# Hybrid decoder trunk: the splitting of the down projection's weights planned ahead, and two additions of squares moved from GpSimd to VectorE

## The chip, the cores and the metric

The kernel runs on one core of a Trainium2 chip. The time is the device time of one execution in microseconds. Before the change the median of 3 runs is 2677.97 us (2677.93 to 2678.42). One more execution was profiled; all durations come from that one.

The engines are called as in the profile: PE (TensorE, matmul), PEld (its weight loads), DVE (VectorE), ACT (ScalarE), POOL (GpSimd) and SP (SyncE, which here only starts DMAs; its queue is SPq).

## The reference

Two layers over 1024 tokens of width 1024. Each is a mixer (attention, gates, output projection) and a gated feed-forward part; a last RMSNorm follows. The part that matters here is the feed-forward one:

```python
h2 = rmsnorm(x, norm2[l])
up = h2 @ w_up[l]                         # 1024 -> 2 x 2816
a, v = up[..., :D_FF], up[..., D_FF:]
a = causal_depthwise_conv(a, conv_w[l], conv_b[l])   # width 3
x = x + (jax.nn.gelu(a, approximate=False) * v) @ w_down[l]   # 2816 -> 1024
```

and the first RMSNorm of the next layer, which needs the mean of the squares of `x` over its 1024 features. All is float32.

## The kernel before

**Numbers in two parts.** Every float32 operand of a matmul is kept as a high and a low part: ACT casts the high part (`split`, L134), DVE subtracts it from the original to get the low part (L139), and PE does three matmuls for each product (high x high, high x low, low x high). A "weight piece" below is one 128x512 block of weights in these two parts.

**Blocks with seven products.** The up and the down projection multiply 2x2 blocks with seven products in place of eight (Strassen's scheme in Winograd's form). It needs sums and differences of weight blocks (on POOL and DVE) and of the gated activations.

**The up projection** runs over 22 units `j`, each 128 of the 2816 features: seven products on PE, then `conv` (an ACT pass, two DVE passes L1338 and L1339, and a GELU on ACT), `gated` (DVE, L1364), differences on POOL (L1369), and `spill`: each result is split (tile `g`, DVE L139) and stored to memory (`gd`), seven stores for each pair of units. Of the last unit these parts are written into the first steps of the down projection, through `at(...)`, which runs them so many turns later.

**The down projection** (`down`) runs over 28 steps `s`: four groups of 2, 2, 3 and 4 pieces of the inner dimension, times seven products `k`. So group 0 is steps 0 to 6 and group 1 steps 7 to 13. In each step:
- `load_g` fetches activations (`gd_in`) some steps ahead; `load_raw` fetches raw weights (`wd_raw`, 1 MB each) at steps 3, 7 and 14 for the following group;
- `prep(s)` prepares weight pieces up to three steps ahead: POOL's L1601 and L1604, DVE's L1605 and L1608 form the sums and differences, and `split` makes the two parts, in buffers `w_hi`/`w_lo` (four) or, from group 1 on, `wd` (tag `p4`, four);
- `product_of(s, e)` for four output blocks `e`: the matmuls (L1630 to L1632, 6 to 12 of 512 columns) into a PSUM bank, and then DVE adds the bank into `x` (L1638).

Steps with `k` = 1, 2, 3 accumulate into the banks that the step before has used, and `k` = 6 into those of `k` = 5. So the first matmul of a block there must wait until DVE has added that block of the step before.

The four `p4` buffers are shared at this place by the last unit's conv tile `cv` (held until its last spill), by the spills' `g` (held until the store has ended) and by `wd`.

**The norm between the layers.** `norm_add` squares a block of `x` on ACT (L424) and adds it to a running sum (L426). The addition is DVE's for every third block and POOL's for the others, unless the argument `adds` says which. In `enter`, `second()` runs the last two steps (`k` = 5 and 6) for the second half of the tokens; after them PE sums over features with `nrm_t` matmuls (L473), behind the next layer's value projection (`v_ps`).

**What sets the order.** PE's order is the written one everywhere. For ACT, DVE and POOL it is the written one within the up projection and in what step 0 of the down projection issues up to its first block; further on, a planner at build time simulates the program and gives each engine, of the instructions that are ready, the one with the lowest number. The number is the place in the program; inside `tc.high_priority(offset=AHEAD)` an instruction counts as if written 200 instructions (`AHEAD`) earlier. An instruction that needs a buffer which is taken waits, and others pass it. On the chip each engine then follows its fixed order. Before the change the additions into `x` (L1638) have this priority, and nothing of `prep` has it.

Of the kernel before, what the change touches and what calls it, by code (L numbers as in the profile page):

```python
# [7 lines left out]
F32R = mybir.dt.float32r  # L8
# [7 lines left out]
P = 128  # L16
# [3 lines left out]
HF = 512  # L20
# [27 lines left out]
AHEAD = 200  # L48
# [3 lines left out]
def f32(ap):  # L52
    return ap.bitcast(F32)
# [3 lines left out]
def trunk_kernel(ctx, tc, x, norm1, w_in, b_gate, w_br, w_o, norm2, w_up, conv_w, conv_b, w_down, norm_f, out, depth=None, probe=None):  # L57
    nc = tc.nc
    act, dve, pe, pool = nc.scalar, nc.vector, nc.tensor, nc.gpsimd
# [4 lines left out]
    sb = ctx.enter_context(tc.tile_pool(name="sb", bufs=1))  # L64
# [56 lines left out]
    def small(name, dtype=F32):  # L121
        return sb.tile([P, 512], dtype, tag="pt", bufs=PT, name=name)
# [8 lines left out]
    def split(hi, lo, src, turn=None):  # L131


        one = act.copy(hi, src)  # L134
        if turn == "is":
            LAST["act"] = one.ins.name
        elif turn == "waits" and LAST:
            tc.add_manual_dep(one.ins, LAST["act"], NO_SYNC, reason="in turn")
        two = dve.tensor_tensor(lo, src, f32(hi), ALU.subtract)  # L139
        if turn == "is":  # L140
            LAST["dve"] = two.ins.name
# [31 lines left out]
    def drive(side, main, ratio, lead=0):  # L173

        due = 0.0
        for _ in range(lead):
            next(main, 0)
        for _ in side:
            due += ratio
            while due >= 1.0:  # L180
                due -= 1.0
                if next(main, 0) == 0:
                    due = -1e9
        for _ in main:
            pass
# [213 lines left out]
    def xc(n, e, sub=slice(0, HF)):  # L399
        return X[n][e // 4][:, e % 4, sub]  # L400

    def x_move(n, out):
        for h in range(2):
            there = xs[n][:, 4 * h : 4 * h + 4, :]
            nc.sync.dma_start(*((there, X[n][h]) if out else (X[n][h], there)))
# [11 lines left out]
    def norm_add(n, e, first=False, sub=slice(0, HF), adds=None):  # L417

        if first:
            ACC[n] = sb.tile([P, HF], F32, tag="ql", bufs=2, name="nrm")  # L420
        acc = ACC[n]
        acc = acc[:, sub]
        sq = acc if first else small("sq")[:, sub]
        act.activation(sq, xc(n, e, sub), AF.Square)  # L424
        if not first:
            (adds or (dve if e % 3 == 1 else pool)).tensor_tensor(acc, acc, sq, ALU.add)  # L426
# [40 lines left out]
    def norm(n, gain, tag, then=None, keep=False):  # L467
        acc = ACC[n]
        ss = sb.tile([P, 8], F32, tag="ss", bufs=2, name="ss")
        yield  # L470
        tot = bank(tag, "nrm_t")
        for c in range(4):
            pe.matmul(tot[:, c : c + 1], acc[:, c * P : (c + 1) * P], ones, start=True, stop=True, skip_group_check=True)  # L473
        yield
        act.activation(ss[:, 0:4], tot[:, 0:4], AF.Sqrt, bias=eps[:, 0:1], scale=1.0 / D)
        dve.reciprocal(ss[:, 4:8], ss[:, 0:4])
        if then:
            table(then, ss[:, 4:5])
        yield
        rb = bank(tag, "nrm_b")  # L480
        for c in range(4):
            pe.transpose(rb[:, c * P : (c + 1) * P], ss[:, 4 + c : 5 + c].to_broadcast([P, P]), ident)
        yield
        new_h(n)
        for e in range(KD):
            hf = kept_f32(n, e) if keep else small("hf")
            dve.scalar_tensor_tensor(hf, xc(n, e), gain[:, e : e + 1], rb, ALU.mult, ALU.mult)
            hi, lo = H[n][0][:, e, :], H[n][1][:, e, :]
            act.copy(hi, hf)
            (pool if e % 2 and not (keep and n) else dve).tensor_tensor(lo, hf, f32(hi), ALU.subtract)  # L490
            if e < KD - 1:
                yield
# [79 lines left out]
    def head(l):  # L572


        def place(n, name):
            x = [big(name, F32R) for _ in range(n)]
            return ([x[0][:, h, :] for h in range(2)] if n == 1 else [y.rearrange("p a b -> p (a b)") for y in x])

        wv = weights(w_in[l][:, OFF_VB : OFF_VB + 256], 256, place(2, "v_w")) if l else early.pop("wv")
        others = lambda: [weights(w_in[l][:, off : off + P], P, place(1, "kq_w")) for off in (OFF_KB, OFF_QB)]  # L580
        if l:
            wk, wq = others()
        yield
        vt = R["vb"] = new_v("vb")
        kt = R["kb", 0] = big("kt", F32R)
        q = R["qb", 0] = new_q()
        if l:
            yield from values_part(vt, wv, range(2))
        else:
            yield from values_part(vt, wv, range(1))  # L590
            wk, wq = others()
            yield from values_part(vt, wv, range(1, 2))
        for n in range(2):
            yield from keys_half(kt, wk, n)
            yield from queries_half(q, wq, n, SCALE)
            if n == 0 and not l:
                yield from values_part(vt, wv, range(2, 4))
        if l:
            yield from values_part(vt, wv, range(2, 4))
# [319 lines left out]
    def piece(src, turn=None):  # L919
        hi = sb.tile([P, 512], F32R, tag="wh", bufs=4, name="w_hi")  # L920
        lo = sb.tile([P, 512], F32R, tag="wl", bufs=4, name="w_lo")
        split(hi, lo, src, turn)
        return hi, lo
# [385 lines left out]
    def ffn(l, pending, final):  # L1309
# [237 lines left out]
        def down(box):  # L1547
# [31 lines left out]
            def place(s, g):  # L1579

                used = [tag for v in range(s, state["w"] + 1) for tag, _ in ws.get(v, ())]
                for tag in ("p4", "w") if g else ("w",):
                    if used.count(tag) < 4:
                        return tag

            def prep(s, most=3):

                while state["w"] < min(s + most, count):
                    v = state["w"]
                    g, k = flat[v]  # L1590
                    m = GROUPS[g]
                    used = [tag for u in range(s, v) for tag, _ in ws[u]]
                    room = 4 - used.count("w") + (4 - used.count("p4") if g else 0)
                    if room < m or (g, m - 1) not in raws:
                        return
                    ws[v] = []
                    for i in range(m):
                        a11, a12, a21, a22 = raws[g, i]
                        if k == 0:
                            temps[i] = small("wd_s")  # L1600
                            pool.tensor_tensor(temps[i], a11, a21, ALU.subtract)  # L1601
                            src = a11
                        elif k == 1:
                            pool.tensor_tensor(a21, a21, a22, ALU.add)  # L1604
                            dve.tensor_tensor(a11, a21, a11, ALU.subtract)  # L1605
                            src = a11
                        elif k == 6:
                            dve.tensor_tensor(a11, a12, a11, ALU.subtract)  # L1608
                            src = a11
                        else:  # L1610
                            src = {2: temps[i], 3: a22, 4: a12, 5: a21}[k]
                        tag = place(s, g)
                        if tag == "p4":
                            w = sb.tile([P, 2, HF], F32R, tag="p4", bufs=4, name="wd")
                            w = (w[:, 0, :], w[:, 1, :])
                            split(*w, src)
                        else:
                            w = piece(src)
                        ws[v].append((tag, w))
                    state["w"] += 1  # L1620

# [27 lines left out]
            for _ in range(READY - 3):  # L1649
                yield  # L1650
            prep(0, 1)
            yield
            yield
            for s, (g, k) in enumerate(flat):
# [8 lines left out]
                elif s == 14:  # L1663
                    for i in range(3):
                        load_raw(3, i, "e8")
                    load_raw(3, 3, "ql")
                prep(s)
                main, other = ("t", "o"), ("ps", "s")
                if g % 2:
# [40 lines left out]
    def enter(l):  # L1710


        def go(rest):
            x_move(0, True)
            heads[l] = [head(l)]
            next(heads[l][0])

            def second():
                for k in (5, 6):
                    for e in range(4):  # L1720
                        yield from rest(k, e)
                        norm_add(1, e + 4 * (k == 5), k == 5 and e == 0)

            drive(norm(0, g1[:, 0, :], "t"), second(), SECOND, 3)
            x_move(1, True)
            return norm(1, g1[:, 0, :], "s", AF.Sigmoid)

        return go
# [271 lines left out]
```

## Time and profile before

| | |
|---|---|
| median of 3 runs | 2677.97 us |
| the profiled execution's own time | 2679.46 us |
| its span in the profile | 2677.4 us |
| granted TensorE clock | 0.999 |
| busy: PE, PEld | 2654.8 us (99%), 2228.7 us (83%) |
| busy: DVE, ACT, POOL | 2031.8 (76%), 1352.3 (51%), 643.7 us (24%) |
| down projection, first layer | from 1129.76 us on |
| down projection, second layer | from 2451.58 us on |
| DMA in group 0, first layer (1129.76 to 1169.50) | 346 GB/s, 94% of the engines' time |

How to read the lines in this text: a timeline row has the start in us from the start of the span, the duration in us, the engine, the line of the kernel, the operation, the tile written and the tiles read, the shape, and in square brackets the idle time before it and what ended it. A row of waits has who waited for whom, the us in total, the number of times and the longest. A row of a stretch has its borders and length, then busy us and number of instructions for PE, PEld, DVE, ACT and POOL, the granted clock, the share of DMA and GB/s. Matmuls are pipelined, so that their recorded durations overlap.

### The profile page before, as it was taken

The page shows a single profiled execution, that of the slowest core. Times are in us where ns is not written, and L with a number is a line of the kernel's source. Part 1 is how long each engine was busy: PE and PEld are TensorE (multiplying, and loading weights), DVE is VectorE, ACT ScalarE, POOL GpSimd, SP SyncE. Part 2 cuts the span into 40 slices and gives each one's busy share as a digit, 9 for nine tenths or more (in the row PEclk, how much of TensorE's full clock was granted, in tenths as well). Part 3 has the DMA queues.
Part 4 walks back from the last instruction along what each step waited for, and adds up shares of the span by engine and source line. Part 5 has one row for each costly group of instructions (what it writes and reads, how often), then busy time and mean ns, then how long its engine had stood idle before and what let it go on. Part 6 is the DMA issues. An engine that isn't in the chain of part 4 may idle for free.

```text
span 2677.4 us, 36661 instructions
## 1 busy us (share of the span) xinstructions
PE 2654.8 (99%) x13080; PEld 2228.7 (83%) x13080; DVE 2031.8 (76%) x3089; ACT 1352.3 (51%) x2494; POOL 643.7 (24%) x467
## 2 busy tenths in 40 slices
PE   9999999999999999999999999999999999999999
PEld 8988888888888888888889888888788888888888
DVE  6777756685888988897658777566858888898865
ACT  6656645464545554532435565455635555554225
POOL 1003211122233443321210041111321344343210
PEclk9999999999999999999999999999999999999999
DMA  5212178573244444688411122785732544446863
GB/s 182 56 55 87 49 196 248 192 251 109 78 138 152 166 141 152 225 317 317 160 36 44 48 79 88 216 246 182 231 95 71 165 150 148 159 157 249 335 249 119
DMA packets 364354, 424.19 MB, mean 158 GB/s; under 512 B 20756, under 2 KB 293516, under 8 KB 362124
## 3 DMA queue, kind: packets, MB, share of 16 engines
q1 hardware_dynamic: 364156, 421.85, 47.9%
q8 instruction: 103, 1.69, 0.3%
q14 instruction: 79, 0.65, 0.1%
q10 hardware_dynamic: 16, 0.00, 0.0%
HBM read 278.07 MB, written 143.72 MB: 158 GB/s over the span
## 4 chain that ended last, share of the span: by engine, by line
PE 88%; DVE 6%; DMA 2%; ACT 2%; issue 1%; POOL 0%; DVEq 0%; SPq 0%; ACTq 0%; POOLq 0%
PE u_a L928 5%; PE u_a L930 5%; PE u_a L929 5%; PE d_ps L1630 5%; PE d_ps L1631 5%; PE d_ps L1632 5%; PE i_a L928 3%; PE u_c L928 3%; PE u_c L930 3%; PE u_c L929 3%; PE i_a L929 3%; PE i_a L930 2%; PE o_ps L166 2%; PE o_ps L168 2%; PE o_ps L167 2%; PE g_ps L166 2%
## 5 line engine op out<-in xcount | busy, mean ns | idle before, releaser
L139 DVE TENSOR_TENSOR w_lo<-up_a,w_hi 128x512 fp32r<-128x512 f32 x240 | 236.9, 994 | 20.5 <-ACT w_hi L134 20.5
L134 ACT CAST w_hi<-up_a 128x512 fp32r<-128x512 f32 x240 | 149.4, 622 | 184.9 <-PE u_a L929 45.8
L1638 DVE TENSOR_TENSOR x<-x,d_ps 128x512 f32<-128x512 f32 (+1 forms) x228 | 152.4, 673 | 77.7 <-PE d_ps L1632 76.5
L1369 POOL TENSOR_TENSOR cv<-cv 128x512 f32<-128x512 f32 x88 | 131.8, 1508 | 249.4 <-DVE cv L1364 139.5
L139 DVE TENSOR_TENSOR g<-cv,g 128x512 fp32r<-128x512 f32 x154 | 151.3, 984 | 5.3 <-ACT g L134 2.8
L139 DVE TENSOR_TENSOR w_lo<-w_raw,w_hi 128x512 fp32r<-128x512 f32 x144 | 110.3, 769 | 56.4 <-ACT w_hi L134 56.0
L134 ACT CAST w_hi<-w_raw 128x512 fp32r<-128x512 f32 x144 | 89.4, 621 | 115.8 <-PE o_ps L167 67.3
L139 DVE TENSOR_TENSOR w_lo<-in_a,w_hi 128x512 fp32r<-128x512 f32 x120 | 90.6, 755 | 60.0 <-ACT w_hi L134 54.5
L134 ACT CAST w_hi<-in_a 128x512 fp32r<-128x512 f32 x120 | 74.5, 621 | 118.3 <-PE i_c L929 49.0
L1630 PE MATMUL d_ps<-gd_in,w_hi 128*128 128x512 f32 (+1 forms) x340 | 130.5, 384 | 1.3 <-ACT w_hi L134 0.6
L1632 PE MATMUL d_ps<-gd_in,w_lo 128*128 128x512 f32 (+1 forms) x340 | 130.0, 382 | 0.0
L1631 PE MATMUL d_ps<-gd_in,w_hi 128*128 128x512 f32 (+1 forms) x340 | 129.9, 382 | 0.0
L928 PE MATMUL u_a<-hh,w_hi 128*128 128x512 f32 x320 | 124.8, 390 | 0.8 <-DVE u L1520 0.8
L928 PE MATMUL u_a<-t_hi,w_hi 128*128 128x512 f32 x320 | 124.7, 390 | 0.0
L929 PE MATMUL u_a<-hl,w_hi 128*128 128x512 f32 x320 | 124.7, 390 | 0.0
L930 PE MATMUL u_a<-hh,w_lo 128*128 128x512 f32 x320 | 124.7, 390 | 0.0
L930 PE MATMUL u_a<-t_hi,w_lo 128*128 128x512 f32 x320 | 124.7, 390 | 0.0
L929 PE MATMUL u_a<-t_lo,w_hi 128*128 128x512 f32 x320 | 124.6, 390 | 0.0
L134 ACT CAST g<-cv 128x512 fp32r<-128x512 f32 x154 | 94.9, 616 | 42.0 <-POOL cv L1369 29.4
L658 DVE TENSOR_TENSOR_SCAN stay<-stay,zero 128x512 f32<-128x512 f32 (+2 forms) x96 | 93.5, 974 | 28.7 <-ACT stay L645 28.1
L1630 PE MATMUL d_ps<-gd_in,wd 128*128 128x512 f32 (+1 forms) x292 | 114.0, 390 | 0.0
L1632 PE MATMUL d_ps<-gd_in,wd 128*128 128x512 f32 (+1 forms) x292 | 112.9, 387 | 0.0
(410 smaller groups left out, 8609.7 us busy)
## 6 DMA issues: line engine op xcount, KB each, us to landing
gd<-g SPq DMA_DIRECT2D x154, 512.0 KB, 3.3
gd_in<-gd SPq DMA_DIRECT2D x154, 512.0 KB, 6.5
up_a<-in_w_up_dram SPq DMA_DIRECT2D x80, 512.0 KB, 5.2
t_kq<-tk SPq DMA_DIRECT2D x32, 768.0 KB, 5.7
wd_raw<-in_w_down_dram SPq DMA_DIRECT2D x22, 1024.0 KB, 7.3
w_raw<-in_w_in_dram SPq DMA_DIRECT2D x80, 256.0 KB, 3.2
in_a<-in_w_in_dram SPq DMA_DIRECT2D x40, 512.0 KB, 4.9
gin<-gs SPq DMA_DIRECT2D x32, 512.0 KB, 4.2
```

What stands on the lines that cost most here:

```text
L134: one = act.copy(hi, src)
L139: two = dve.tensor_tensor(lo, src, f32(hi), ALU.subtract)
L166: pe.matmul(o, lh, rh, start=(first and i == 0), stop=False, skip_group_check=share)
L658: one = dve.tensor_tensor_scan(rev, rev, zero[:, 0:1].to_broadcast([P, c1 - c0]), 1.0 if c1 == L else sv[:, c1 : c1 + 1], ALU.mult, ALU.add)
L928: pe.matmul(o, w[0][:, c], rh, start=(first and i == 0), stop=False, skip_group_check=True)
L929: pe.matmul(o, w[0][:, c], rl, start=False, stop=False, skip_group_check=True)
L930: pe.matmul(o, w[1][:, c], rh, start=False, stop=(last and i == 3), skip_group_check=True)
L1369: return lambda: pool.tensor_tensor(dst, a, b, ALU.subtract)
L1630: pe.matmul(o[:, sub], wh[:, c], gh[:, sub], start=(i == 0 and k in (0, 4, 5)), stop=False, skip_group_check=True)
L1631: pe.matmul(o[:, sub], wh[:, c], gl[:, sub], start=False, stop=False, skip_group_check=True)
L1632: pe.matmul(o[:, sub], wl[:, c], gh[:, sub], start=False, stop=(i == m - 1), skip_group_check=True)
L1638: dve.tensor_tensor(x, x, o[:, sub], ALU.add)
```

## The change

The splitting of the down projection's weights into two parts (a cast on ACT, a subtraction on DVE) gets the same priority of 200 places; the indented lines are otherwise the same. The sums and differences of weight blocks before it (L1601, L1604, L1605, L1608) stay outside. In `enter`, for the norm between the layers, the additions of squares of the last two blocks of the last step (`k` = 6, `e` = 2 and 3) go to DVE; by the rule for every third block both were POOL's.

```diff
+from contextlib import nullcontext
...
                         tag = place(s, g)
-                        if tag == "p4":
-                            w = sb.tile([P, 2, HF], F32R, tag="p4", bufs=4, name="wd")
-                            w = (w[:, 0, :], w[:, 1, :])
-                            split(*w, src)
-                        else:
-                            w = piece(src)
+                        with tc.high_priority(offset=AHEAD) if True else nullcontext():
+                            if tag == "p4":
+                                w = sb.tile([P, 2, HF], F32R, tag="p4", bufs=4, name="wd")
+                                w = (w[:, 0, :], w[:, 1, :])
+                                split(*w, src)
+                            else:
+                                w = piece(src)
                         ws[v].append((tag, w))
...
-                        norm_add(1, e + 4 * (k == 5), k == 5 and e == 0)
+                        norm_add(1, e + 4 * (k == 5), k == 5 and e == 0, adds=dve if k == 6 and e > 1 else None)
```

## The prediction

> **What bounds the kernel now.** I read the page's busy table first, then the list of who waited for whom on PE, then the busy time by stretches, and last the timelines of PE, DVE, ACT and POOL around each place where PE waits in the code that the diff touches.
>
> ```profile
> span 2677.4 us, 36661 instructions
> ...
> PE 2654.8 (99%) x13080; PEld 2228.7 (83%) x13080; DVE 2031.8 (76%) x3089; ACT 1352.3 (51%) x2494; POOL 643.7 (24%) x467
> ```
>
> ```profile
> PE br_ps L166 <- DVE gin L1284: 2.5, 3, 1.2
> ...
> PE d_ps L1630 <- ACT w_hi L134: 0.6, 2, 0.3
> PE nrm_t L473 <- POOL nrm L426: 0.5, 1, 0.5
> ```
>
> ```profile
> 1129.76:1169.50 39.74, 38.91 (x169) 31.31 (x168) 39.51 (x57) 15.55 (x25) 10.55 (x7) 1.00 0.94 346
> ...
> 1207.60:1264.70 57.10, 57.10 (x253) 47.33 (x252) 40.37 (x59) 15.05 (x26) 11.65 (x8) 1.00 0.84 313
> ```
>
> ```profile
> L1638 DVE TENSOR_TENSOR x<-x,d_ps 128x512 f32<-128x512 f32 x26 | 17.5, 680 | 0.2
> ```
>
> PE is busy for 99% of the span, and its waits in the code of the change are tenths of a microsecond. So whatever this change can win is small, and a loss needs a new stall. The rows, in order: the page's span and busy times; three of PE's waits (us in total, times, longest); two stretches of the program; and the additions into x within the first of these. The two rows of stretches (length, then PE, PEld, DVE, ACT, POOL busy) hold the main point. In the first, group 0 of the down projection of the first layer (steps 0 to 6), DVE is busy for 39.51 of 39.74 us: for this stretch VectorE, and not PE, sets the pace. In group 2, with three weight pieces to a step, DVE is at 40.37 of 57.10 and an order among its instructions costs nothing. The second layer repeats the first.
>
> What those waits cost is read best from the starts of successive matmuls, because a recorded matmul (0.39 us) is longer than the distance to the next.
>
> ```profile
> 1134.74 0.39 PE L1631 MATMUL d_ps<-gd_in,w_hi 128*128 128x512 f32 x1
> 1134.97 0.39 PE L1632 MATMUL d_ps<-gd_in,w_lo 128*128 128x512 f32 x1
> 1135.65 0.47 PE L1630 MATMUL d_ps<-gd_in,w_hi 128*128 128x512 f32 x1 [0.29 <-ACT w_hi L134]
> ...
> 1162.75 0.39 PE L1632 MATMUL d_ps<-gd_in,w_lo 128*128 128x512 f32 x1
> 1163.55 0.47 PE L1630 MATMUL d_ps<-gd_in,w_hi 128*128 128x512 f32 x1 [0.41 <-issue]
> ...
> 1164.78 0.40 PE L1632 MATMUL d_ps<-gd_in,w_lo 128*128 128x512 f32 x1
> 1165.31 0.50 PE L1630 MATMUL d_ps<-gd_in,w_hi 128*128 128x512 f32 x1
> ...
> 1348.22 0.28 PE L167 MATMUL v_ps<-v_w,hh 128*128 128x256 f32 x1
> 1348.34 0.28 PE L168 MATMUL v_ps<-v_w,hl 128*128 128x256 f32 x1
> 1349.11 1.05 PE L473 MATMUL nrm_t<-ones,nrm 128*128 128x1 f32 x8 [0.49 <-POOL nrm L426]
> ...
> 2456.80 0.39 PE L1632 MATMUL d_ps<-gd_in,w_lo 128*128 128x512 f32 x1
> 2457.47 0.47 PE L1630 MATMUL d_ps<-gd_in,w_hi 128*128 128x512 f32 x1 [0.29 <-ACT w_hi L134]
> ...
> 2486.02 0.39 PE L1632 MATMUL d_ps<-gd_in,w_lo 128*128 128x512 f32 x1
> 2486.54 0.50 PE L1630 MATMUL d_ps<-gd_in,w_hi 128*128 128x512 f32 x1
> ```
>
> An undisturbed matmul follows after 0.23 us (1134.74 to 1134.97). The excess is 0.68 - 0.23 = 0.45 at step 1, 0.80 - 0.23 = 0.57 and 0.53 - 0.23 = 0.30 at step 6, together 1.32 in the first layer. In the second it is 0.44 and 0.29, together 0.73. The 256-wide matmuls follow after 0.12, so the norm's sum waits 0.77 - 0.12 = 0.65. All that the diff could remove is therefore 1.32 + 0.73 + 0.65 = 2.70 us, 0.1% of the span.
>
> **The change, part by part.** No instruction is added or removed but two that change engine. First, the splitting of the down projection's weights: the casts on ACT (L134) and the subtractions on DVE (L139) get the same 200 places that the additions into x (L1638) have. The sums and differences before them (L1601 and L1604 on POOL, L1605 and L1608 on DVE) stand outside the block and keep their number. The split instructions pass the convolution, the GELU and the spills of the last up unit, and also those additions into x that are written behind them.
>
> ```profile
> 1132.48 1.27 DVE L1339 SCALAR_TENSOR_TENSOR cv<-u,cw,cv 128x1022 f32<-128x1022 f32 x1
> 1133.67 0.68 DVE L1638 TENSOR_TENSOR x<-x,d_ps 128x512 f32<-128x512 f32 x1
> 1134.27 0.68 DVE L139 TENSOR_TENSOR w_lo<-wd_raw,w_hi 128x512 fp32r<-128x512 f32 x1
> 1134.87 1.88 DVE L1638 TENSOR_TENSOR x<-x,d_ps 128x512 f32<-128x512 f32 x3
> ...
> 1159.77 0.68 DVE L139 TENSOR_TENSOR g<-cv,g 128x512 fp32r<-128x512 f32 x1
> ...
> 1162.77 0.68 DVE L1638 TENSOR_TENSOR x<-x,d_ps 128x512 f32<-128x512 f32 x1
> 1163.37 0.68 DVE L139 TENSOR_TENSOR w_lo<-wd_raw,w_hi 128x512 fp32r<-128x512 f32 x1
> 1163.97 0.68 DVE L139 TENSOR_TENSOR wd<-wd_raw,wd 128x512 fp32r<-128x512 f32 x1
> 1164.57 0.68 DVE L1638 TENSOR_TENSOR x<-x,d_ps 128x512 f32<-128x512 f32 x1
> ```
>
> Step 1. The gap at 1135.65 is put down to ACT, but the cast that the w_lo of 1134.27 reads was over by then; PE starts 0.1 us after a DVE addition (the second, 1134.87 + 0.60, as 1163.37 to 1163.97 shows one DVE operation taking 0.60 of the queue). My reading is that output block 0's addition, written behind step 1's weights by hand, had to let another block's addition (1133.67) pass ahead of the second w_lo (1134.27). With equal priority the w_lo comes first, everything behind it moves up by 0.60, and the 0.45 goes: in both layers 0.89. I take this as likely to happen.
>
> Step 6. Four additions a step, 26 in the stretch: the one at 1162.77 is the 21st, block 0 of step 5. Step 6 accumulates into the same banks, so the matmul at 1163.55 must wait for it (1162.77 + 0.68 = 1163.45), and the one at 1165.31 for the 22nd (1165.25). These times are fixed by how much DVE work is queued ahead, since DVE has no idle time from 1129.76 on (0.23 us in all). So the 0.45 that PE gains at step 1 is waited for again at step 6, and is worth nothing there unless DVE gets less to do before these additions. That is the step I weigh most: step 1 nets 0, and not -0.89.
>
> What can leave the queue ahead of them are spills (g, 1159.77: 0.60 each, not read before group 3), because the weights take their buffers first:
>
> ```profile
> 1158.24 0.62 ACT L134 CAST wd<-wd_raw 128x512 fp32r<-128x512 f32 x1 [0.66 <-DMA gd<-g]
> ...
> 1160.48 0.62 ACT L134 CAST wd<-wd_raw 128x512 fp32r<-128x512 f32 x1 [0.50 <-DVE g L139]
> ```
>
> ```profile
> 1155.71 1.29 POOL L1601 TENSOR_TENSOR wd_s<-wd_raw 128x512 f32<-128x512 f32 x1 [5.21 <-DMA wd_raw<-in_w_down_dram]
> ```
>
> Here wd waits, and g before it, for the same four buffers (tag p4) until an earlier g has been written to memory. With the new priority the last two spills can lose to step 7's weights: up to 2 x 0.60 = 1.2 us less ahead of the 22nd addition, the gain's bound. What can pass the 21st are step 6's second w_lo and step 7's wd (1163.37, 1163.97): it ends 1.2 later, block 0 of step 6 starts at 1164.75 and block 1, six matmuls of 0.23 on, at 1166.1 in place of 1165.31, a loss of 0.8. The 22nd itself already stands behind both. So step 6 moves by -1.2 to +0.8 in a layer; I take the middle, -0.2, since the queue is full whichever comes first: -0.4 in both layers. SP: no load is moved by hand; the spills' stores come later with their casts, and nothing on the queue behind them reads them before group 3. A weight block that lands late (POOL waited 5.21 us for it) limits how early step 7's second piece can go. Groups 2 and 3 have DVE time to spare, so I cost the edit there at nothing; were it full, the price would be 0.60 per addition passed.
>
> Second, the two additions of squares.
>
> ```profile
> 1346.29 0.68 DVE L1638 TENSOR_TENSOR x<-x,d_ps 128x512 f32<-128x512 f32 x1
> 1347.00 0.63 ACT L424 ACTIVATE sq<-x 128x512 f32<-128x512 f32 x1 [1.38 <-DVE x L1638]
> 1347.78 1.28 POOL L426 TENSOR_TENSOR nrm<-nrm,sq 128x512 f32<-128x512 f32 x1 [2.56 <-ACT sq L424]
> ```
>
> The last one ends the chain x, square, sum, matmul at 1349.11. On DVE it takes 0.68 for 1.28: -0.60 of the 0.65 wait. The one before it costs DVE 0.60 while DVE waits for loads, so nothing on the path; were it queued ahead of 1346.29 it would cost its 0.60 and leave no gain. I take -0.60.
>
> The Trainium skill (SBUF — State Buffer, section SBUF: two separate sides) says that a VectorE operation with two SBUF inputs and a GpSimd operation lock each other out for a whole instruction. The trace has such longer times: 1.62 for a subtraction whose like take 0.68 (the row of 1177.76 further down). By that rule taking POOL's additions away would also shorten DVE's subtractions beside them, the norm would give its whole 0.65, and the sum would be less by 0.05.
>
> Sum: step 1 -0.89, given back at step 6 +0.89, step 6's own -0.4, norm -0.60: -1.0 us. The profiled execution took 2679.46 us around its 2677.4 of span, 1.5 above the median of 2677.97; against that median the sum gives 2677.0.
>
> **The rivals.** First, the change does all that its words say: PE's waits at steps 1 and 6 go as well. For it speaks that spills leave the queue; against it that DVE is at 39.51 of 39.74. Time: 2677.97 - 2.70 = 2675.3.
>
> Second, on the other side: the spills starve. If step 7's two pieces and step 8's first hold three of the four p4 buffers while the last conv tile holds the fourth until its last spill, then step 8's second piece gets a buffer only when step 7 is nearly over.
>
> ```profile
> 1174.28 0.39 PE L1630 MATMUL d_ps<-gd_in,wd 128*128 128x512 f32 x1
> ...
> 1175.64 0.39 PE L1630 MATMUL d_ps<-gd_in,wd 128*128 128x512 f32 x1
> 1177.76 1.62 DVE L139 TENSOR_TENSOR wd<-wd_raw,wd 128x512 fp32r<-128x512 f32 x1
> ```
>
> Step 7's first piece is read last before 1174.28. Then come a cast of 0.62, up to three queued operations of 0.60 and a subtraction of 0.68 to 1.62: ready at 1175.6 to 1178.3, wanted at 1175.64 + 2 x 0.23 = 1176.1. So it costs 0 to 2.2 us in a layer, 4.4 in both; with step 6's worst case (2 x 0.8) and the norm's gain, 4.4 + 1.6 - 0.6 = +5.4, 2683.4. It decides from the moment at which three weight pieces have p4 buffers and one spill has none. That weights and spills already wait for one another there speaks for it; that the second block's load lands late, so that the spills may slip in, speaks against. A row of such waits is what the Trainium skill (Perfetto Trace Analysis, section Optimization Strategy) would put down to too few buffers, a gap that comes back on an engine that should be full; by it a new order leaves the gaps, and this rival with its 2683.4 gains on the first.
>
> Third, the planner, fed other times, orders the next layer's mixer otherwise. The longest single wait of PE in the list is 1.2 us (for gin, in the mixer); one such wait more or less is its price, 2675.8 or 2678.2 with the sum above.
>
> **How the numbers follow.** My sum has 0.45, with its own range 2675.6 to 2679.2 (step 6 at -1.2 or +0.8 in one layer and half of it in the other, the norm's 0.60 kept at the low end and lost at the high one); the first rival 0.22, the starved spills 0.25, the third 0.08. The time is that of the likeliest, 2677.0. The range goes from 2674.9, just under the first rival, to 2682.5, within the second, of which some 0.10 lies above. A measurement of this kernel tells about 0.2%, 5.4 us, from no change. Faster than 2672.6 is out of reach of the 2.70 found: 0.03, left to the third rival, whose single wait may be several. Slower than 2683.3: half of the second, since its 2683.4 has step 8 alone and step 11 has the same pair of pieces, 0.12, and 0.03 of the third: 0.15. Within: 0.82.
>
> **What would show it.** Right: no gap at step 1, a gap of much the same sum at step 6, DVE full up to step 8, the nrm_t matmul straight behind v_ps with a DVE addition of 0.68 ahead of it. Wrong on the fast side: no gap at step 6 and spills' g behind its additions. Wrong on the slow side: PE waiting at steps 8 or 11 for a wd cast or subtraction, which waited for a buffer from step 7, or a wait of DVE for a block that has not landed.

## The result and the profile after

| | before | after |
|---|---|---|
| median | 2677.36 us (2674.94 to 2679.99, 22 runs) | 2680.53 us (2677.78 to 2685.97, 22 runs) |
| ratio | 1 | 1.0012, interval 1.0007 to 1.0018 |
| profiled execution, its span | 2679.46, 2677.4 us | 2680.04, 2677.9 us |

The change makes the kernel slower by 3.2 us (1.9 to 4.8 by the interval). I had forecast 2677.0, a gain of 1.0, in a range from 2674.9 to 2682.5. The measured time lies in the range and within 0.2% of before, but the sign is the other one.

The runs spread over 5 us before and 8 us after, and in the two profiled executions parts of the program that the change does not touch differ by some 2 us. So the traces are compared by stretches: the table gives distances in time on PE, from the first matmul of the down projection to step 6 and to step 14 (the end of group 1), and the sum of the gaps in between (a distance of two matmuls less the undisturbed 0.23 us, where this is over 0.09).

| | step 6 at, layer 1 / 2 | step 14 at, layer 1 / 2 | gaps by step, layer 1 | gaps by step, layer 2 |
|---|---|---|---|---|
| before | 33.79 / 33.21 | 77.84 / 77.25 | 1: 0.45; 6: 0.57, 0.30, 0.11 | 1: 0.45; 6: 0.29, 0.11 |
| after | 35.50 / 35.69 | 80.76 / 79.33 | 3: 0.12; 5: 0.30, 0.11; 6: 2.20, then 8 of 0.2 | 3: 0.11; 5: 0.41, 0.11, 0.11; 6: 2.20 |

The gap of step 1 is gone in both layers. In its place step 6 has one of 2.20 us. The page of the kernel after, its span and busy times:

```profile
span 2677.9 us, 36660 instructions
...
PE 2655.1 (99%) x13080; PEld 2230.4 (83%) x13080; DVE 2036.9 (76%) x3091; ACT 1352.4 (51%) x2494; POOL 640.2 (24%) x465
```

What PE waited for in the kernel after (us in total, times, longest). The waits put down to "issue" went from 0.4 us, once, to 4.1, twice; POOL is gone from the rows of the norm.

```profile
PE d_ps L1632 <- issue: 4.1, 2, 2.0
...
PE nrm_t L474 <- DVE nrm L427: 0.2, 1, 0.2
```

PE's timeline of the kernel after, around the places that the prediction showed: step 1, step 6 and the norm in the first layer, step 6 in the second.

```profile
1132.77 0.39 PE L1634 MATMUL d_ps<-gd_in,w_lo 128*128 128x512 f32 x1
1132.99 0.39 PE L1632 MATMUL d_ps<-gd_in,w_hi 128*128 128x512 f32 x1
...
1160.62 0.39 PE L1634 MATMUL d_ps<-gd_in,w_lo 128*128 128x512 f32 x1
1163.06 0.47 PE L1632 MATMUL d_ps<-gd_in,w_hi 128*128 128x512 f32 x1 [2.04 <-issue]
...
1349.06 0.28 PE L169 MATMUL v_ps<-v_w,hl 128*128 128x256 f32 x1
1349.18 1.04 PE L474 MATMUL nrm_t<-ones,nrm 128*128 128x1 f32 x8
...
2483.31 0.39 PE L1634 MATMUL d_ps<-gd_in,w_lo 128*128 128x512 f32 x1
2485.74 0.47 PE L1632 MATMUL d_ps<-gd_in,w_hi 128*128 128x512 f32 x1 [2.04 <-issue]
```

At step 1 the next matmul follows after 0.22, so nothing waits. At step 6 it follows after 2.44 and 2.43 us. The norm's matmul follows after 0.12: its 0.65 is gone. What step 6 waits for stands in DVE's timeline of the kernel after:

```profile
1139.25 3.20 DVE L140 TENSOR_TENSOR w_lo<-wd_raw,w_hi 128x512 fp32r<-128x512 f32 x2
...
1159.27 0.68 DVE L140 TENSOR_TENSOR wd<-wd_raw,wd 128x512 fp32r<-128x512 f32 x1
1159.87 0.68 DVE L1640 TENSOR_TENSOR x<-x,d_ps 128x512 f32<-128x512 f32 x1
1160.47 1.28 DVE L140 TENSOR_TENSOR w_lo<-wd_raw,w_hi 128x512 fp32r<-128x512 f32 x2
1161.67 0.68 DVE L140 TENSOR_TENSOR wd<-wd_raw,wd 128x512 fp32r<-128x512 f32 x1
1162.27 1.28 DVE L1640 TENSOR_TENSOR x<-x,d_ps 128x512 f32<-128x512 f32 x2
```

The 21st addition (block 0 of step 5) is the first half of the row of 1162.27; it leaves the queue at 1162.87, and PE goes on at 1163.06. Ahead of it now stand both w_lo of step 6 and both pieces of step 7, three of them in a row. Before, the order was w_lo, addition, w_lo, wd, addition. PE waits for an addition while DVE prepares pieces that PE needs only at step 7. (The pieces of steps 6 and 7 are both written at the start of step 5, ahead of that step's additions.)

The stretches of group 0 of the kernel after, the first and the second layer, and between them four microseconds at the start of the first layer's step 6 (borders, length, busy PE, PEld, DVE, ACT, POOL, granted clock, DMA share, GB/s):

```profile
1127.55:1170.23 42.68, 40.50 (x169) 32.48 (x168) 42.59 (x60) 15.53 (x25) 10.55 (x7) 0.96 0.94 346
...
1164.00:1168.00 4.00, 4.00 (x12) 3.15 (x12) 4.00 (x8) 0.62 (x1) 0.00 (x0) 0.57 1.00 404
...
2450.04:2491.30 41.26, 38.98 (x170) 31.24 (x169) 41.26 (x58) 14.21 (x23) 10.54 (x7) 1.00 0.91 334
```

DVE is busy from end to end in both, and group 0 is longer than the 39.74 us of before. The middle row is the other difference between the layers: the granted clock was 0.57 in the mean of these four microseconds, and the eight gaps of 0.2 (1.57 us together) are matmuls in that time.

### The profile page after: what moved, and what is told of

Read it like the earlier page. It is cut to its first block, busy times and chain, and to the rows that moved or that the text cites. A ratio compares the mean times of both kernels' runs of the same rounds, so it can differ in the third digit from the quotient of the medians.

```text
span 2677.9 us, 36660 instructions
## 1 busy us (share of the span) xinstructions
PE 2655.1 (99%) x13080; PEld 2230.4 (83%) x13080; DVE 2036.9 (76%) x3091; ACT 1352.4 (51%) x2494; POOL 640.2 (24%) x465
## 4 chain that ended last, share of the span: by engine, by line
PE 91%; DVE 5%; DMA 1%; ACT 1%; issue 1%; POOL 0%; DVEq 0%; SPq 0%; ACTq 0%
PE u_a L929 5%; PE u_a L931 5%; PE u_a L930 5%; PE d_ps L1632 5%; PE d_ps L1634 5%; PE d_ps L1633 5%; PE i_a L929 3%; PE u_c L931 3%; PE u_c L929 3%; PE u_c L930 3%; PE i_a L930 3%; PE i_a L931 2%; PE o_ps L167 2%; PE o_ps L168 2%; PE o_ps L169 2%; PE g_ps L167 2%
## 5 line engine op out<-in xcount | busy, mean ns | idle before, releaser
L135 ACT CAST wd<-wd_raw 128x512 fp32r<-128x512 f32 x64 | 39.5, 622 | 147.7 <-DVE x L1640 68.8
L1632 PE MATMUL d_ps<-gd_in,wd 128*128 128x512 f32 (+1 forms) x292 | 114.0, 390 | 0.0
```

The costliest lines, as they stand in the source:

```text
L1632: pe.matmul(o[:, sub], wh[:, c], gh[:, sub], start=(i == 0 and k in (0, 4, 5)), stop=False, skip_group_check=True)
```

## The experiments

All short diffs are against the kernel after, unless they say otherwise. The same two distances and the sum of the gaps up to step 14 are given for each; the gap of the norm was 0.64 to 0.67 in every run without the second part of the change, and 0.00 to 0.02 in every run with it.

### The two parts one by one

Priority alone (prio_only), the additions of squares alone (norm_only), and priority for the pieces of step 1 alone (step1_only):

```diff
 prio_only
-norm_add(1, e + 4 * (k == 5), k == 5 and e == 0, adds=dve if k == 6 and e > 1 else None)
+norm_add(1, e + 4 * (k == 5), k == 5 and e == 0)
 norm_only: the kernel before with
+adds=dve if k == 6 and e > 1 else None
 step1_only: prio_only with
-with tc.high_priority(offset=AHEAD) if True else nullcontext():
+with tc.high_priority(offset=AHEAD) if v == 1 else nullcontext():
```

> The priority for the splits alone; the squares stay as before. Theory of the queue (step 6's first matmul waits for VectorE's 21st addition, and the planned order has 26 other VectorE operations ahead of it from the last convolution on where before has 24): step 6 starts some 35.5 to 35.7 us after step 0 in both layers (before 33.79 and 33.22), with one gap of about 2.2 us ahead of it; step 14 starts some 1.5 to 2 us later after step 0 than before (77.84 and 77.26); nrm_t keeps its gap of 0.65; whole time +3 to +4 us against before. Theory of the buffers (spills starved of p4): a gap at step 8 or 11. If only the squares or the clock made the loss: no difference from before.

> The two additions of squares alone on VectorE; the weights as before. Every theory: steps 0 to 14 as before (77.84 and 77.26 us), the gap ahead of nrm_t in the middle of the program gone (0.65 to under 0.1); whole time -0.6 us, less than these runs can tell. If the squares made the loss: +3 us.

> The priority only for step 1's two weight pieces; squares as before. The planned order has step 1's low part ahead of the additions, as in the changed kernel, and 24 operations ahead of the 21st addition, as before. Theory of the queue: the gap of 0.45 at step 1 is gone and the same time is waited again at step 6 (gap 0.57 grows to about 1.0); step 14 starts 77.8 and 77.3 us after step 0, within 0.2 of before; whole time unchanged. Rival: the gain of step 1 is kept, step 14 starts 0.45 us earlier in each layer and the whole time falls by 0.9 us.

The fourth of these runs keeps the whole change, but has the additions into `x` stay ahead of the pieces:

```diff
 adds_first
-                with tc.high_priority(offset=AHEAD):
+                with tc.high_priority(offset=2 * AHEAD):
                     dve.tensor_tensor(x, x, o[:, sub], ALU.add)
```

> The changed kernel, with the additions into x given 400 places in place of 200, so that the splits pass convolution and spills but no addition. 24 operations are ahead of the 21st addition, as before. Theory of the queue: step 6 starts 33.2 to 33.8 us after step 0, as before, the loss is gone; gap at step 1 back; whole time that of before less 0.6 for the norm. If passing convolution and spills made the loss, it stays at +3 us.

| | median, before beside it | ratio and interval | step 6 at | step 14 at | gaps, layer 1 / 2 |
|---|---|---|---|---|---|
| prio_only | 2679.80, 2676.29 | 1.0014, 1.0005 to 1.0023 | 35.20 / 35.23 | 78.85 / 78.87 | 2.43 / 2.44 |
| norm_only | 2676.29, 2676.29 | 1.0000, 0.9991 to 1.0009 | 33.76 / 34.23 | 77.81 / 78.30 | 1.40 / 1.86 |
| step1_only | 2675.67, 2676.29 | 0.9999, 0.9991 to 1.0008 | 33.39 / 33.40 | 77.45 / 77.45 | 1.14 / 1.16 |
| adds_first | 2676.03, 2676.29 | 0.9998, 0.9989 to 1.0006 | 33.69 / 33.41 | 77.74 / 77.47 | 1.34 / 1.07 |

The loss is the priority's: alone it costs 3.5 us (1.3 to 6.2). The additions of squares take the 0.65 away in the trace, which a whole time with an interval of 2.4 us to either side can't show. Steps 6 and 14 come a little earlier in prio_only than I expected. With the additions ahead again (adds_first) the loss is gone, but so is the gain of step 1: the gap there is 0.45 again. So the pieces' priority harms only by its rank against the additions into `x`.

step1_only is the look at step 1. Its gap is gone in both layers, and step 6 waits 0.72 in the first layer and 0.74 in the second, where before had 0.57 and none. PE's timeline of step1_only (the row names ACT, but it starts 0.1 us after the end of the 21st addition, 1160.64 + 0.68):

```profile
1160.48 0.39 PE L1634 MATMUL d_ps<-gd_in,w_lo 128*128 128x512 f32 x1
1161.42 0.47 PE L1632 MATMUL d_ps<-gd_in,w_hi 128*128 128x512 f32 x1 [0.56 <-ACT w_hi L135]
```

The gaps of both layers come to 2.30 us; before had 2.29 and adds_first 2.41, norm_only 3.26. The last three have the same order there and still spread by 1 us, so these sums alone do not tell whether step 1's gain is kept. Step 14 came 0.39 earlier than before in the first layer and 0.20 later in the second; I had expected no difference. What spreads the kernels, and what is left of the gain without it, stands at the end of the experiments on POOL below.

### Which work stands ahead of the addition

The planner's order can be counted: of all that DVE does from the last conv on, other than additions into `x`, how many operations stand ahead of the 21st and the 22nd addition. Before, adds_first, norm_only and step1_only have 24 and 26; after and prio_only have 26 and 26. Both that passed the 21st are the ones that the prediction names, step 6's second w_lo and step 7's wd. Four kernels were to change this count. early_pieces gives no priority to step 7 and later; after_defer is the kernel after with step 7's subtractions held behind the 22nd addition; spills_late is norm_only with the last two spills written later; defer_spills has the priority for step 1 alone, the hold, the late spills and the squares on DVE.

```diff
 early_pieces: prio_only with
+with tc.high_priority(offset=AHEAD) if v < 7 else nullcontext():
 after_defer
+        if "after" in LAST:
+            tc.add_manual_dep(two.ins, LAST["after"], NO_SYNC, reason="behind the addition")
...
+                    if v == 7 and s == 5:
+                        return
+                    if v == 7:
+                        LAST["after"] = state["x"]
...
+                if (s, e) == (5, 1):
+                    state["x"] = one.ins.name
 spills_late: norm_only with
-            later = ... (3, 5, 7, 9, 11) if j == NF - 1 else ...
+            later = ... (3, 5, 7, 17, 19) if j == NF - 1 else ...
```

> The priority for the pieces of steps 0 to 6 alone (step 7's wd and all later ones as before); squares as before. One operation less passes the 21st addition: 25 are ahead of it, 24 before the change, 26 with all pieces. Theory of the queue, one VectorE operation being 0.60 of the queue: step 6 starts half way, some 34.3 to 34.9 us after step 0 (33.4 to 33.8 with 24, 35.2 with 26), its gap is about 1.6, step 14 starts at +78.2 (77.45 with 24, 78.85 with 26). If a wait for the p4 buffers of step 7's pieces made the loss, it is gone here: 77.5.

> The changed kernel, but step 7's two subtractions are held behind the addition of step 5, block 1. The priority stays; 24 operations are ahead of the 21st addition and 24 ahead of the 22nd (26 in the kernel before and in the changed one). Theory of the queue: the gap of 2.2 falls to about 1.0 or less, step 14 starts at +77.5 or earlier. If the priority of the splits costs in another way (their casts, the buffers), the gap stays near 2.2.

> The kernel before with the squares on VectorE and the last unit's last two spills written eight turns later, without the priority. A test of what the prediction named as the possible gain (spills leaving the queue ahead of step 6). The planned order still has 24 operations ahead of the 21st addition, because step 7's and step 8's pieces move up into the spills' places. Theory of the queue: steps 6 and 14 start as before, +33.4 to 33.8 and +77.5. If fewer spills ahead are a gain by themselves: -1.2 us in each layer.

> The theory of the queue used the other way round: step 1's priority alone, the squares on VectorE, the last two spills eight turns later, and step 7's two subtractions held behind the addition of step 5, block 1, so that they cannot take the spills' places. 22 operations are ahead of the 21st and the 22nd addition (24 and 26 before). Expected: no gap at step 1, step 6's gaps (1.0 in sum) gone or nearly, step 14 at +76.2 to 76.6 in both layers, no gap at nrm_t; in sum 2.5 to 3.5 us less than before, about 0.1%. If other waits take over (a weight piece of step 7 or 8 too late), step 14 stays at +77.4.

| | count | step 6 at | step 14 at | gaps, layer 1 | gaps, layer 2 |
|---|---|---|---|---|---|
| prio_only | 26, 26 | 35.20 / 35.23 | 78.85 / 78.87 | 6: 2.21 | 6: 2.21 |
| early_pieces | 25, 26 | 34.58 / 34.58 | 78.19 / 78.35 | 6: 1.60 | 6: 1.61 |
| after_defer | 24, 24 | 33.92 / 33.99 | 77.53 / 79.00 | 6: 1.12 | 6: 0.96; 9: 1.24 |
| spills_late | 24, 26 | 33.45 / 33.21 | 78.32 / 78.05 | 1: 0.45; 6: 0.23, 0.30; 8: 0.68 | 1: 0.45; 6: 0.30; 8: 0.60 |
| defer_spills | 22, 22 | 32.64 / 32.67 | 76.63 / 76.35 | 8: 0.33 | 8: 0.11 |

(Gaps of 0.11 beside larger ones are left out.) One operation fewer ahead, from prio_only to early_pieces, and step 6 begins 0.62 and 0.65 us earlier and waits 0.61 less: the price of one operation in a full queue, 0.60. Two fewer, in after_defer, take 1.08 and 1.24 from the 2.20 of the kernel after. spills_late shows why taking work away need not help. The two spills went, but the count stayed 24: the planner filled their places with step 7's and step 8's subtractions. And with the spills later a new gap appears at step 8, 0.6 to 0.7 in both layers, which I did not follow further.

defer_spills is the one that gets both: no gap at step 1 and none at step 6. Its timelines of DVE and of PE:

```profile
1158.16 1.28 DVE L1648 TENSOR_TENSOR x<-x,d_ps 128x512 f32<-128x512 f32 x2
1159.35 1.28 DVE L140 TENSOR_TENSOR wd<-wd_raw,wd 128x512 fp32r<-128x512 f32 x2
```

```profile
1159.95 0.39 PE L1642 MATMUL d_ps<-gd_in,w_lo 128*128 128x512 f32 x1
1160.17 0.39 PE L1640 MATMUL d_ps<-gd_in,w_hi 128*128 128x512 f32 x1
```

The additions of blocks 0 and 1 stand ahead of step 7's two subtractions, and step 6 begins without a wait. Step 14 is reached 1.2 and 0.9 us earlier than before. With the norm's 0.65 that makes 2.8 us in the trace. The whole time, 2676.21 us beside 2676.59 of before (ratio 0.9997, 0.9988 to 1.0006), is the same within what can be measured; by the interval it lies between 3.2 us faster and 1.6 slower, so that the 2.8 is neither confirmed nor excluded. No version here beats the kernel before beyond its interval. after_defer (2676.68), early_pieces (2680.16) and spills_late (2677.48) have one time each, beside the same 2676.59.

The 1.24 at step 9 of after_defer is in one layer only. There two subtractions for pieces took 3.40 us in place of 1.28, ahead of the addition that PE waits for, while POOL was at work; subtractions beside POOL are the subject of the next part.

### Two subtractions in a row beside POOL

Two passes of 0.60 explain 1.20. But from step1_only to prio_only step 6 moves by 1.81 and 1.83. DVE's timeline shows another difference at step 3. First prio_only, then step1_only, then POOL in step1_only:

```profile
1139.69 3.19 DVE L140 TENSOR_TENSOR w_lo<-wd_raw,w_hi 128x512 fp32r<-128x512 f32 x2
1142.80 0.68 DVE L1640 TENSOR_TENSOR x<-x,d_ps 128x512 f32<-128x512 f32 x1
1143.40 0.68 DVE L140 TENSOR_TENSOR g<-cv,g 128x512 fp32r<-128x512 f32 x1
```

```profile
1139.75 1.47 DVE L140 TENSOR_TENSOR w_lo<-wd_raw,w_hi 128x512 fp32r<-128x512 f32 x1
1141.14 0.68 DVE L1640 TENSOR_TENSOR x<-x,d_ps 128x512 f32<-128x512 f32 x1
1141.74 1.20 DVE L140 TENSOR_TENSOR w_lo<-wd_raw,w_hi 128x512 fp32r<-128x512 f32 x1
1142.86 0.68 DVE L140 TENSOR_TENSOR g<-cv,g 128x512 fp32r<-128x512 f32 x1
```

```profile
1139.37 3.02 POOL L1370 TENSOR_TENSOR cv<-cv 128x512 f32<-128x512 f32 x2 [12.68 <-DVE cv L1365]
```

The same three DVE operations, two subtractions and an addition, take 1143.40 - 1139.69 = 3.71 us of the queue in prio_only and 1142.86 - 1139.75 = 3.11 in step1_only, 0.60 less. Both run beside POOL's two differences of the last unit. A subtraction reads two tiles in SBUF and is stretched there, 0.68 to 1.47 and 1.20; an addition into `x` reads a PSUM bank and keeps its 0.68. Between two stretched subtractions the addition costs nothing; behind them it costs its 0.60. The Trainium skill (SBUF — State Buffer, section SBUF: two separate sides) has a DVE operation with two SBUF inputs and a GpSimd operation lock each other out for a whole instruction, and the rows agree with it, the untouched addition included.

Two runs separate this from the passes, and a third looks at it at another place:

```diff
 not_step3: prio_only with
+with tc.high_priority(offset=AHEAD) if v != 3 else nullcontext():
 only_1_3: prio_only with
+with tc.high_priority(offset=AHEAD) if v in (1, 3) else nullcontext():
 defer_pool: defer_spills with the spills as before, and
-                            dve.tensor_tensor(a11, a12, a11, ALU.subtract)
+                            (pool if g == 0 else dve).tensor_tensor(a11, a12, a11, ALU.subtract)
```

> The priority for all pieces but step 3's; squares as before. 26 operations stay ahead of the 21st addition, but step 3's two subtractions are apart again, with an addition into x between them, as before the change. In the run with the priority alone these two ran one behind the other beside POOL's differences and took 3.19 us in all, in the run with step 1's priority alone 1.47 and 1.20, apart. If it is that overlap with POOL that makes the loss larger than 2 x 0.60: step 6 starts at +34.6 (35.2 with all pieces) and step 14 at +78.2 (78.85). If the overlap costs nothing in the end: unchanged at +35.2 and +78.85.

> The complement: the priority for steps 1 and 3 alone, so that 24 operations are ahead of the 21st addition, and step 3's two subtractions follow each other beside POOL's differences. If the overlap costs 0.6: step 6 at +34.0 (33.4 with step 1 alone), step 14 at +78.0 (77.45). If not: as with step 1 alone.

> Another way to have 22 operations ahead of the 21st and 22nd addition: step 1's priority alone, squares on VectorE, step 7's subtractions held behind step 5's second addition, and group 0's two differences for k = 6 on POOL in place of VectorE; the spills stay where they were. Expected by the theory of the queue: no gap at steps 1 and 6 and step 14 at +76.3 to 76.6, if POOL's two more operations do not lengthen VectorE's beside them; with that, up to 1 us later. Whole time 2 to 3 us less than before, about the limit of what these runs tell.

Where step 6 begins, in layer 1 and layer 2:

| | step 7's and step 6's pieces do not pass | they pass |
|---|---|---|
| step 3's subtractions apart | 33.39, 33.40 (step1_only) | 34.52, 34.01 (not_step3) |
| step 3's subtractions in a row | 34.15, 34.56 (only_1_3) | 35.20, 35.23 (prio_only) |

Step 3 costs 0.76 and 1.16 in the first column and 0.68 and 1.22 in the second. The passes cost 1.13 and 0.61 above, 1.05 and 0.67 below. But each cell is one execution, and executions with one and the same order differ by as much: step 6 begins at 33.21 to 34.23 in before, norm_only and adds_first. The two middle kernels have one whole time each, 2679.26 and 2680.05 beside 2679.14 of before, which can't tell them apart.

What spreads them is a second meeting of DVE with POOL. When the second block of group 1's weights has landed, POOL runs L1601 and L1604, and in both layers of every kernel compared here two DVE operations beside them are stretched. POOL starts on it between 22.5 and 26.0 us after step 0, so that they are other operations each time, by other amounts. DVE in the kernel before, first layer (POOL starts at 1155.71) and second (at 2476.38):

```profile
1155.77 1.78 DVE L139 TENSOR_TENSOR w_lo<-wd_raw,w_hi 128x512 fp32r<-128x512 f32 x1
...
1158.07 1.18 DVE L1608 TENSOR_TENSOR wd_raw<-wd_raw 128x512 f32<-128x512 f32 x1
...
2477.59 1.19 DVE L139 TENSOR_TENSOR w_lo<-wd_raw,w_hi 128x512 fp32r<-128x512 f32 x1
...
2479.30 1.19 DVE L1608 TENSOR_TENSOR wd_raw<-wd_raw 128x512 f32<-128x512 f32 x1
```

What the two take of the queue beyond 0.60 each is 1.61 us in the first layer here and 1.02 in the second; over the kernels of this table it is 1.0 to 2.2. With that taken off, the start of step 6 depends on the order alone:

| | beyond 0.60, layer 1 / 2 | step 6 at, less that |
|---|---|---|
| before | 1.61 / 1.02 | 32.18 / 32.19 |
| norm_only | 1.57 / 2.04 | 32.18 / 32.20 |
| adds_first | 1.50 / 1.22 | 32.19 / 32.20 |
| step1_only | 1.60 / 1.61 | 31.79 / 31.79 |
| only_1_3 | 1.75 / 2.15 | 32.40 / 32.41 |
| not_step3 | 1.55 / 1.01 | 32.97 / 33.00 |
| prio_only | 1.60 / 1.63 | 33.60 / 33.60 |
| after | 1.91 / 2.10 | 33.60 / 33.59 |

So step 3's two subtractions in a row cost 0.61, the two passes 1.2, and step 1's priority gains 0.40, in both layers: together 1.41 later than before.

The gain of step 1 is thus kept for the most part, against my expectation: in the first layer, where POOL's part is alike (1.61 and 1.60), step 6's gap grew only from 0.57 to 0.72. DVE was not full at steps 1 and 2 of the kernel before; it waited there for PE's late blocks. Its starts show it, 0.78 apart in before for a pair that step1_only has 0.60 apart:

```profile
1137.92 0.69 DVE L139 TENSOR_TENSOR w_lo<-wd_s,w_hi 128x512 fp32r<-128x512 f32 x1
1138.70 0.69 DVE L1638 TENSOR_TENSOR x<-x,d_ps 128x512 f32<-128x512 f32 x1
```

defer_pool (2678.01 beside 2679.14, ratio 0.9996, 0.9987 to 1.0005; count 22 and 22; step 6 at 33.65 and 33.63, step 14 at 77.25 and 77.15) gives two of DVE's differences to POOL. There is no gap at step 6, but one of 0.90 at step 1. The difference on POOL ran beside the last conv pass on DVE. The timeline of POOL, then of DVE, in defer_pool:

```profile
1130.52 1.68 POOL L1616 TENSOR_TENSOR wd_raw<-wd_raw 128x512 f32<-128x512 f32 x1 [3.63 <-DVE w_lo L140]
```

```profile
1130.97 2.31 DVE L1342 SCALAR_TENSOR_TENSOR cv<-u,cw,cv 128x1022 f32<-128x1022 f32 x1
1133.20 0.68 DVE L140 TENSOR_TENSOR w_lo<-wd_raw,w_hi 128x512 fp32r<-128x512 f32 x1
```

The conv pass took 2.31 where it takes 1.27 undisturbed, and step 1's second w_lo came 1 us later. Work that goes from DVE to POOL comes back in part as longer DVE operations.

## Why the prediction was right and wrong

**Right: what bounds the stretch.** DVE was nearly full in group 0 and stayed so (42.59 of 42.68 and 41.26 of 41.26 us). The gaps at steps 1 and 6 followed the order of its queue and what POOL stretched in it, in every kernel that was run.

**Right in part: step 1.** The gap went in both layers because the second w_lo came ahead of another block's addition. But "step 1 nets 0" was wrong in size: in step1_only, at an equal part of POOL, step 6 starts 0.40 earlier in a layer and only the rest of the 0.45 is given back. "DVE has no idle time" (0.23 us) was read from the idle column; by the starts DVE lost some 0.5 us at steps 1 and 2 in waits for PE.

**Right: the norm.** 0.65 to nothing, the term of 0.60. In the whole time it can't be seen.

**Right: which operations would pass.** Step 6's second w_lo and step 7's wd passed the 21st addition, and block 0 of step 6, which I had put 1.2 later by them, in fact starts 1.41 later in prio_only in the first layer, 2.02 in the second (where POOL's part is 0.61 larger than before).

**Wrong: "So step 6 moves by -1.2 to +0.8 in a layer; I take the middle, -0.2".** This is the step that failed, and at three points.

- The gain side was empty. The spills, "up to 2 x 0.60 = 1.2 us less", did not leave: in the kernel after they stand where they stood in DVE's order, and the two operations that passed come on top. ACT's timeline of the kernel after has a spill's cast still ahead of step 7's first piece, which then waits until the store of an earlier spill has freed a buffer:

```profile
1152.93 0.62 ACT L135 CAST g<-cv 128x512 fp32r<-128x512 f32 x1 [2.83 <-POOL wd_s L1602]
1154.72 0.62 ACT L135 CAST wd<-wd_raw 128x512 fp32r<-128x512 f32 x1 [1.16 <-DMA gd<-g]
```

  And where they were made to leave (spills_late), other pieces took their places. The condition "unless DVE gets less to do" was the right one, and I let a change of order stand for it.
- The loss side had both passes, with their 0.60 each, and was treated as an edge. The diff itself says that the pieces get the additions' priority, and the pieces are written ahead of them: the pass was the rule and not the bad case. Taking +0.8 in both layers, with the norm's -0.60, gives +1.0 and the right sign.
- The loss at step 3 was not in the working at all. I looked at the order only where PE already waited. The row of a subtraction stretched to 1.62 beside POOL stood in the prediction, but I asked of it only what less work on POOL would free, and not what two of them in a row would cost: 0.6 us of the queue in a layer, by the rows and by the runs.

In place of the -0.2 that I took, the order moved step 6 by 2 x 0.60 + 0.61 - 0.40 = +1.41 us in a layer. Step 14 moves by 1.0 only, because before had two more gaps within step 6 (0.30 and 0.11), which the large one takes in. From step 14 to the projection's last matmul nothing differs (134.9 and 139.7 us, in the kernels before and after alike), as the prediction had it for groups 2 and 3.

That makes 2.0 us for the priority in both layers, or 1.4 with the norm's 0.65: less than the 1.9 to 4.8 that were measured. The traces as they stand, with POOL's part as it fell in each, give more: against the three kernels with the order of before (before, norm_only, adds_first: step 14 at 155.1 to 156.1 for both layers together) prio_only has 157.7, a loss of 1.6 to 2.6 us, and the kernel after, less the 1.57 at the low clock, 158.5, a loss of 2.4 to 3.4. Less the norm's 0.65 that is 1.8 to 2.8 for the whole change. Measured are 3.2. So the sign and about half of the loss are accounted for by the order. The rest is not shown. It may be POOL's part, which differs from one execution to the next, and falls of the clock like the one described at the end, which took 1.57 us of the profiled execution.

**The rivals.** The first (all gaps go, 2675.3) did not come: of the large gaps only those of step 1 and the norm went. It takes defer_spills to make step 6's go. The second had the sign right and the mechanism wrong: no gap appeared at step 8 or 11, and no buffer starved. It was the additions that paid, which I had priced ("0.60 per addition passed") for groups where DVE has time to spare, and not for the one where it has none. The third, another order in the mixer: PE's wait for `gin` went from 2.5 to 1.6 us, but prio_only has 2.3, so I read nothing into it.

## What to carry to other kernels

On an engine that is full, a priority creates no time; it only chooses who waits. So count the operations that will stand ahead of the one for which the bounding engine waits, and price each at its share of the queue (here 0.60 us). A gap closed early in the stretch is kept only as far as the full engine itself stood waiting there (here 0.40 of 0.45), and that is read from the starts of its operations, not from its busy time. What frees a buffer (an addition out of PSUM) should not rank below what prepares for later steps, and what is put off must be held explicitly, because a planner that takes the first ready instruction fills the place with something equally early.

When an order moves, look for neighbours too: two operations that another engine stretches are cheaper with one between them that it does not. And before a difference between two executions is put down to the order, check what varies within one order; here that was 1 us in a layer, from the moment at which POOL started on a block of weights.

## What was not expected of the hardware

The clock fell in the first layer of the profiled execution after. Behind the 2.2 us gap, from 1164 to 1168, the mean granted clock was 0.57, and matmuls followed each other at 0.43 in place of 0.23 us, 1.57 us in all:

```profile
1165.39 0.63 PE L1634 MATMUL d_ps<-gd_in,w_lo 128*128 128x512 f32 x1
1165.82 0.63 PE L1632 MATMUL d_ps<-gd_in,w_hi 128*128 128x512 f32 x1
```

The same gap of 2.20 in the second layer, and both gaps of 2.21 in prio_only, were not followed by such a fall. So a gap of this length does not cause it each time, and whether it had a part in it is open. The mean clocks on record for the other executions suggest that such falls were more frequent in the two kernels with gaps of 2.2 us: of 33 executions of after and prio_only, 8 have 1.000 and 4 have 0.998, among them the slowest of each; of 33 executions of norm_only, step1_only and adds_first, 23 have 1.000 and none has 0.998. These figures are rounded to 0.001, which is 2.7 us of this span, so they do not show how many falls there were or what they cost.

A subtraction of 0.68 us took up to 1.8 beside POOL, and two in a row 3.2 to 3.4, while additions that read PSUM kept 0.67 to 0.68 beside the same POOL operations.
